# Strassen-style weight sums by accumulating DMAs, and a 32-byte place for the first weight tile, in a two-layer encoder trunk

## The chip, the cores and the metric

The kernel runs on one core of a Trainium2 chip. The metric is the device time of one execution in microseconds (us). Before the change three runs took 2366.21, 2369.56 and 2368.86 us, median 2368.86 us. For a kernel of this length a difference of under 0.2% (about 5 us) can't be told from none.

## What is computed

Two layers; each is a feed-forward block (FFN), a mixer of three branches (banded attention, pooling, forgetting attention) and another FFN, on a sequence of 512 tokens of width 1024, in float32. The change lies in the FFNs:

```python
def swiglu(h, w_gate, w_up, w_down):
    return (jax.nn.silu(h @ w_gate) * (h @ w_up)) @ w_down
...
x = x + 0.5 * mod[:, 2][:, None, :] * swiglu(h, ffn_w_gate[l, 0], ffn_w_up[l, 0], ffn_w_down[l, 0])
```

`w_gate` and `w_up` are 1024x2816, `w_down` is 2816x1024, so that the middle width of 2816 makes 22 units of 128 columns.

## The kernel before

**Products.** Activations lie transposed (features on the 128 partitions, 512 tokens in a row). Every float32 operand is split into a rounded high part (a ScalarE copy, in the traces an ACT `CAST`) and a low part (a VectorE subtraction, a DVE `TENSOR_TENSOR`), and a product is three matmuls: high by high, high by low, low by high. The weights are the stationary operand, loaded anew for each matmul (PEld), the activations the moving one. The split is `split_to` (lines 417 and 418) or, in `wchunk`, lines 310 and 312.

**FFN stages.** The 22 units of an FFN go in three parts, of 6, 8 and 8 units; after each part the part's share of `w_down` follows (`k_outer`, 512 columns wide, and in the last half of the last part 256 wide, "split"). In the first part of an FFN all or four of the six units are made the plain way (512 columns wide, `Ffn.unit`). All others go in pairs by `seven`.

**`seven`.** Two units of `w_gate`, or of `w_up`, make a 1024x256 block, which is cut in 2x2 sub-blocks A11, A12, A21, A22; the activations are cut likewise, in B11 to B22. The Winograd form of Strassen's rule needs seven products of sub-blocks in place of eight, each of four steps of 128 and three matmuls 256 wide: 84 matmuls. For it the weights are summed as S1 = A21 + A22, S2 = S1 - A11, S3 = A11 - A21 and S4 = A12 - S2, and the activations, once for an FFN, as T1 to T4 (class `Blocks`). The products run in the order A11·B11, A12·B21, S2·T2, S1·T1, S3·T3, S4·B22, A22·T4, on three PSUM banks x, y and w. Between them ACT copies a bank out (lines 572, 576, 578, 580) and DVE sums the copies (the `tens` rows of 256 elements). S2·T2, S1·T1, S3·T3 and A22·T4 add to a bank that holds an earlier product, so the copy of the bank must have been made before.

A pair of units is one `seven` for `w_gate` (PSUM tag `acc`), then one for `w_up` (tag `mm`). There are eleven stretches of such work, eight of four pairs (8 calls) and three of a single pair (2 calls), 70 calls in all.

**Loads and buffers.** The two halves of a block come by two DMAs of 512 KB each on SP's queue into `raw` (2 buffers; line 547). DVE makes the four sums of 128x512 (lines 549 and 486) into two `v2` tiles. The splits of A11/A12 and of A22 go into `w` tiles (3 buffers), those of S1/S2 and S3/S4 into two `ptb` tiles (2 buffers). A `ptb` tile is free when PE has made its two products.

**Place.** `duo` puts a weight tile at an offset (`place`, in floats) in its buffer: `WIDE` (0) for 512-wide matmuls, `NARROW` (16 floats, 64 bytes) for 256-wide ones; the `ptb` tiles lie 64 bytes off too, by small pad tiles. The moving operands begin on multiples of 256 bytes.

**Order.** The program is traced in Python, and the framework's scheduler then orders the instructions of each engine by a model of its own; on the chip each engine runs its list strictly in order, and waits for semaphores.

Of the kernel before, what the change touches and what calls it, by code (L numbers as in the profile page):

```python
# [15 lines left out]
F32 = mybir.dt.float32  # L16
F32R = mybir.dt.float32r
I32 = mybir.dt.int32
AF = mybir.ActivationFunctionType
# [3 lines left out]
P = 128  # L23
# [17 lines left out]
def encoder_kernel(tc, xT, c, w_ada, b_ada, gains, w_gate, w_up, w_down, w_qkv, w_f, w_ubg,  # L41
# [374 lines left out]
    def split_to(hi, lo, src):  # L416
        nc.scalar.copy(hi, src)  # L417
        nc.vector.tensor_tensor(lo, src, hi.bitcast(F32), op=ALU.subtract)  # L418


    def k_outer(chunk_src, nch, lhs_rhs, before_last=None):

        if before_last is None:
            parts, nheld = [(None, slice(0, T), [acc() for _ in range(4)])], 2
        else:
            parts = [(hs, slice(hs * HALF, (hs + 1) * HALF), [b((P, HALF)) for _ in range(4)])
                     for hs, b in enumerate((mmt, acc))]
            nheld = 3  # L430

        def go(part, j, chunks):
# [52 lines left out]
    def minus(o, a, b):  # L485
        nc.vector.tensor_tensor(o, a, b, op=ALU.subtract)  # L486

    class Blocks:
# [28 lines left out]

        def t1_t3(self, m):
            b1, b2 = self.full[m], self.full[m + 2]
            minus(b1[:, :, FIRST], b1[:, :, SECOND], b1[:, :, FIRST])  # L520
            minus(b1[:, :, SECOND], b2[:, :, SECOND], b1[:, :, SECOND])

        def t2_t4(self, m):
            b1, b2 = self.full[m], self.full[m + 2]
            minus(b2[:, :, SECOND], b2[:, :, SECOND], b1[:, :, FIRST])
            minus(b2[:, :, FIRST], b2[:, :, FIRST], b2[:, :, SECOND])

        def split(self, q):
            self.parts[q] = blk("b"), blk("b")
# [8 lines left out]
            q0, cols = {"T1": (0, FIRST), "T3": (0, SECOND), "T4": (2, FIRST), "T2": (2, SECOND)}[name]  # L538
            return [tuple(part[:, k % 2, cols] for part in self.parts[q0 + k // 2]) for k in range(4)]

    def seven(srcs, blocks, bank):

        raws = []
        for src in srcs:
            side_work()
            raw = st([P, KD, P], F32, "raw", NRAW)
            last["dma"] = nc.sync.dma_start(raw, src).ins
            raws.append(raw)
        tens = lambda o, a, b, op: nc.vector.tensor_tensor(o, a, b, op=op)
        a11, a12, a21, a22 = raws[0][:, :4], raws[0][:, 4:], raws[1][:, :4], raws[1][:, 4:]  # L550
        ah, al = duo((KD, P), "w", NARROW)
        split_to(ah, al, raws[0])
        bh, bl = duo((4, P), "w", NARROW)
        split_to(bh, bl, a22)
# [24 lines left out]
        go(x, "S3", "T3", False)  # L579
        nc.scalar.copy(c[:, 3], x)  # L580
# [15 lines left out]
    class Ffn:  # L596
# [19 lines left out]
        def act(self, n, pg, pu, sg=None):  # L616
            if sg is None:
                sg = apply([pg], AF.Silu)
            pr = t2(T)
            parts = pu if isinstance(pu, list) else [pu]  # L620
            m = T // len(parts)
            for i, p in enumerate(parts):
                cols = slice(i * m, (i + 1) * m)
                nc.vector.tensor_tensor(pr[:, cols], p, sg[:, cols], op=ALU.mult)
            a = blk("b")
            split_to(a[:, 0, :], a[:, 1, :], pr)
            return a

        def run(self, nxt):
# [4 lines left out]
            for part, (f0, nf) in enumerate(parts):  # L634
# [40 lines left out]
                    n += 1  # L675
                if not opening:
                    blocks.finish()
                while n < nf:
                    both = [apply(p, AF.Silu)
                            for p in seven([w_gate[l, s, f0 + n + i] for i in range(2)], blocks, acc)]  # L680
                    ups = seven([w_up[l, s, f0 + n + i] for i in range(2)], blocks, mmt)
                    for i, sg in enumerate(both):
                        acts.append(self.act(n + i, None, ups[i], sg))
                    n += 2
                MOD_RATE[0] = 1.2
                for c0 in (0, T):
# [644 lines left out]
```

## Time and profile before

| what | value |
|---|---|
| median of three runs | 2368.86 us |
| the profiled execution | 2370.22 us |
| its span on the core | 2368.4 us |
| granted TensorE clock | 1.0 |
| PE, DVE, ACT, POOL busy | 99%, 75%, 51%, 14% of the span |
| calls of `seven` | 70, in eleven stretches |
| read from HBM | 312.16 MB |

The profile is of one execution. A matmul's row begins when it begins; its end is modelled, and matmuls overlap in the pipeline, so that a busy PE says little: the distance from one matmul's start to the next is what it costs. `L418` is line 418 of the kernel, `ptb<-v` a tile of tag `ptb` written from one of tag `v2`; a group's row has its count, busy time, mean duration in ns and the idle time ahead of it, with who ended it.

### The profile page before, as it was taken

How to read it: one execution, taken by the hardware profiler on the slowest of the kernel's cores; microseconds unless marked ns; L12 is line 12 of the kernel's file. 1: busy time of each engine (PE TensorE's matmuls, PEld its weight loads, DVE VectorE, ACT ScalarE, POOL GpSimd, SP SyncE). 2: the span in 40 equal slices, each digit the busy share in tenths (PEclk: the TensorE clock that was granted, in tenths of full speed). 3: DMA queues.
4: the chain of work that ended last, by engine and by line, in shares of the span. 5: the costliest groups of instructions: out<-in, count | busy, mean ns of one | idle time of the engine just before them, and what ended most of it. 6: DMA issues, size and time to landing. Idle time of an engine off the chain costs nothing.

```text
span 2368.4 us, 37435 instructions
## 1 busy us (share of the span) xinstructions
PE 2335.2 (99%) x14322; PEld 2075.8 (88%) x14322; DVE 1770.8 (75%) x3147; ACT 1197.2 (51%) x2097; POOL 326.4 (14%) x433
## 2 busy tenths in 40 slices
PE   7999999999999999999999999999999999999999
PEld 5898998878888898989999989888788888999898
DVE  8887866787686577878687878677866855878583
ACT  5353555676632353635553536456765324636262
POOL 3000011244411100000100000112543211000000
PEclk9999999999999999999999999999999999999999
DMA  8535342333355524353415353533333654143233
GB/s 292 182 107 187 101 167 88 105 99 110 122 199 202 188 71 161 116 187 99 152 63 178 101 185 107 187 107 99 99 122 106 221 199 167 63 142 108 98 100 107
DMA packets 117976, 325.18 MB, mean 137 GB/s; under 512 B 11650, under 2 KB 13826, under 8 KB 117796
## 3 DMA queue, kind: packets, MB, share of 16 engines
q1 hardware_dynamic: 115106, 314.38, 39.9%
q0 software_dynamic: 2688, 8.39, 1.2%
q8 instruction: 113, 1.85, 0.3%
q14 instruction: 67, 0.55, 0.1%
q10 hardware_dynamic: 2, 0.00, 0.0%
HBM read 312.16 MB, written 6.38 MB: 134 GB/s over the span
## 4 chain that ended last, share of the span: by engine, by line
PE 85%; DVE 9%; ACT 3%; DMA 2%; issue 2%; SPq 0%; ACTq 0%; DVEq 0%; POOL 0%; POOLq 0%
PE acc L140 16%; PE acc L142 16%; PE acc L141 16%; PE mm L151 4%; PE mm L149 4%; PE mm L150 4%; PE acc L149 4%; PE acc L151 4%; PE acc L150 4%; PE mm L140 3%; PE mm L142 3%; PE mm L141 3%; PE mm L1020 1%; DVE w L418 1%; DVE v L486 1%
## 5 line engine op out<-in xcount | busy, mean ns | idle before, releaser
L312 DVE TENSOR_TENSOR w<-raw,w 128x1024 fp32r<-128x1024 f32 x247 | 313.2, 1271 | 161.6 <-ACT w L310 161.3
L310 ACT CAST w<-raw 128x1024 fp32r<-128x1024 f32 (+1 forms) x255 | 264.3, 1040 | 273.4 <-PE acc L142 187.5
L140 PE MATMUL acc<-b,w 128*128 128x512 f32 (+1 forms) x960 | 359.8, 375 | 0.0
L141 PE MATMUL acc<-b,w 128*128 128x512 f32 (+1 forms) x960 | 356.3, 371 | 0.0
L142 PE MATMUL acc<-b,w 128*128 128x512 f32 (+1 forms) x960 | 356.1, 371 | 0.0
L142 PEld LDWEIGHTS acc<-b,w 128*128 128x128 f32 x960 | 180.4, 188 | 31.6
L140 PEld LDWEIGHTS acc<-b,w 128*128 128x128 f32 x960 | 180.3, 188 | 30.3
L141 PEld LDWEIGHTS acc<-b,w 128*128 128x128 f32 x960 | 180.6, 188 | 29.8
L417 ACT CAST ptb<-v 128x1024 fp32r<-128x1024 f32 x140 | 146.6, 1050 | 100.8 <-DVE v L486 62.0
L418 DVE TENSOR_TENSOR ptb<-v,ptb 128x1024 fp32r<-128x1024 f32 x140 | 170.7, 1222 | 33.2 <-ACT ptb L417 32.7
L140 PE MATMUL acc<-hhi,w 128*128 128x512 f32 x480 | 191.9, 401 | 2.4 <-ACT hhi L747 1.7
L142 PE MATMUL acc<-hhi,w 128*128 128x512 f32 x480 | 188.8, 393 | 2.6 <-DVE w L312 2.6
L141 PE MATMUL acc<-hlo,w 128*128 128x512 f32 x480 | 188.7, 393 | 0.5 <-DVE hlo L750 0.5
L417 ACT CAST w<-raw 128x1024 fp32r<-128x1024 f32 (+1 forms) x140 | 116.5, 832 | 122.1 <-PE acc L142 56.2
L418 DVE TENSOR_TENSOR w<-raw,w 128x1024 fp32r<-128x1024 f32 (+1 forms) x140 | 133.1, 950 | 13.0 <-ACT w L417 13.0
L140 PE MATMUL acc<-w,hhi 128*128 128x512 f32 x336 | 138.7, 414 | 0.9 <-ACT t L849 0.9
L142 PE MATMUL acc<-w,hlo 128*128 128x512 f32 x336 | 131.9, 392 | 0.0
L141 PE MATMUL acc<-w,hhi 128*128 128x512 f32 x336 | 131.6, 392 | 0.0
L227 DVE CUSTOM_DVE_ANT_0 v<-v,b,badac 128x1024 f32<-128x1024 f32 x87 | 116.8, 1352 | 10.1 <-DMA v<-in_w_ada_dram 10.1
L149 PE MATMUL acc<-b,ptb 128*128 128x256 f32 x420 | 118.3, 282 | 0.0
L150 PE MATMUL acc<-b,ptb 128*128 128x256 f32 x420 | 117.8, 280 | 0.0
L151 PE MATMUL acc<-b,ptb 128*128 128x256 f32 x420 | 117.7, 280 | 0.0
(312 smaller groups left out, 6583.7 us busy)
## 6 DMA issues: line engine op xcount, KB each, us to landing
raw<-in_w_down_dram SPq DMA_DIRECT2D x88, 512.0 KB, 4.1
v<-in_w_ada_dram SPq DMA_DIRECT2D x87, 512.0 KB, 5.1
raw<-in_w_up_dram SPq DMA_DIRECT2D x82, 512.0 KB, 3.6
raw<-in_w_gate_dram SPq DMA_DIRECT2D x79, 512.0 KB, 3.6
b<-in_w_ada_dram SPq DMA_DIRECT2D x57, 512.0 KB, 4.7
raw<-in_w_ubg_dram SPq DMA_DIRECT2D x56, 512.0 KB, 3.6
raw<-in_w_qkv_dram SPq DMA_DIRECT2D x42, 512.0 KB, 3.7
raw<-in_w_branch_dram SPq DMA_DIRECT2D x24, 512.0 KB, 3.7
```

Of the source, the lines that this page charges most:

```text
L140: mm(o, lh, rh, start=start, stop=False)
L141: mm(o, lh, rl, start=False, stop=False)
L142: mm(o, ll, rh, start=False, stop=stop)
L149: mm(o, lh, rh, start=start and k == 0, stop=False, skip_group_check=True)
L150: mm(o, lh, rl, start=False, stop=False, skip_group_check=True)
L151: mm(o, ll, rh, start=False, stop=k == 3, skip_group_check=True)
L227: dot = nc.vector.tensor_tensor_reduce(out=raw, in0=raw, in1=silc[0], scale=1.0, scalar=badac[:, l, j, d:d + 1], op0=ALU.mult, op1=ALU.add ...
L310: nc.scalar.copy(hi, raw)
L312: lo_eng.tensor_tensor(lo, raw, hi.bitcast(F32), op=ALU.subtract)
L417: nc.scalar.copy(hi, src)
L418: nc.vector.tensor_tensor(lo, src, hi.bitcast(F32), op=ALU.subtract)
L486: nc.vector.tensor_tensor(o, a, b, op=ALU.subtract)
```

## The change

**Sums.** The signs are turned so that every weight sum is an addition: S1 = A21 + A22, S2' = S1 + A11, S3' = A11 + A21 and S4' = A12 + S2', with the T's, the SiLU's scale and the product with the second unit turned to match. A11 + A21 and A21 + A22 aren't made by DVE: SP loads A11 a second time, into the `v2` tile of S3' and S4' (`s34`, 256 KB), and A21/A22 into a tile of tag `pta` (`r1`, one buffer) in place of the second `raw`; then two DMAs on GpSimd's queue (POOL) fetch A21 and A22 from HBM once more, and add them in the place where they land (`accum_op`). DVE makes the other two sums, one of them in place in `r1`, and S1/S2' are split from `r1` itself. A call of `seven` now has two DVE sums of 128x512 for four, three SP loads (256 KB, 512 KB, 512 KB) for two, and two adding DMAs of 256 KB.

**Place.** A third place, `ENTRY`, 8 floats (32 bytes), is used for A11/A12 of the first `seven` of each stretch, and for the first chunk of a split `k_outer`; all else stays at 64 bytes.

**Order.** The lists of all engines come out otherwise, as the prediction shows.

```diff
-    WIDE, NARROW = 0, 16
+    WIDE, ENTRY, NARROW = 0, 8, 16
...
-            hi, lo = wchunk(chunk_src(c), (2, T), place=WIDE if before_last is None else NARROW)
+            hi, lo = wchunk(chunk_src(c), (2, T), place=WIDE if before_last is None else NARROW if c else ENTRY)
...
-            minus(b1[:, :, FIRST], b1[:, :, SECOND], b1[:, :, FIRST])
+            minus(b1[:, :, FIRST], b1[:, :, FIRST], b1[:, :, SECOND])
...
-            minus(b2[:, :, SECOND], b2[:, :, SECOND], b1[:, :, FIRST])
-            minus(b2[:, :, FIRST], b2[:, :, FIRST], b2[:, :, SECOND])
+            for half, other in ((SECOND, b1[:, :, FIRST]), (FIRST, b2[:, :, SECOND])):
+                t = b2[:, :, half]
+                nc.vector.scalar_tensor_tensor(t, other, -1.0, t, op0=ALU.mult, op1=ALU.subtract)
...
-    def seven(srcs, blocks, bank):
-
-        raws = []
-        for src in srcs:
-            side_work()
-            raw = st([P, KD, P], F32, "raw", NRAW)
-            last["dma"] = nc.sync.dma_start(raw, src).ins
-            raws.append(raw)
+    def seven(srcs, blocks, bank, place=NARROW):
+
+        top, low = srcs
+        s34 = st([P, 2, 4, P], F32, "v2", 4)
+        side_work()
+        nc.sync.dma_start(s34[:, 0], top[:, :4])
+        r0 = st([P, KD, P], F32, "raw", NRAW)
+        last["dma"] = nc.sync.dma_start(r0, top).ins
+        side_work()
+        r1 = st([P, 2, 4, P], F32, "pta", 1)
+        last["dma"] = nc.sync.dma_start(r1.rearrange("p a k c -> p (a k) c"), low).ins
+        nc.gpsimd.dma_start(s34[:, 0], low[:, :4], accum_op=ALU.add)
+        nc.gpsimd.dma_start(r1[:, 0], low[:, 4:], accum_op=ALU.add)
...
-        s12, s34 = st([P, 2, 4, P], F32, "v2", 4), st([P, 2, 4, P], F32, "v2", 4)
-        tens(s12[:, 0], a21, a22, ALU.add)
-        minus(s34[:, 0], a11, a21)
-        minus(s12[:, 1], s12[:, 0], a11)
-        minus(s34[:, 1], a12, s12[:, 1])
+        tens(r1[:, 1], r1[:, 0], r0[:, :4], ALU.add)
+        tens(s34[:, 1], r1[:, 1], r0[:, 4:], ALU.add)
         pair12, pair34 = duo((2, 4, P), "ptb"), duo((2, 4, P), "ptb")
-        split_to(*pair12, s12)
+        split_to(*pair12, r1)
         split_to(*pair34, s34)
...
+                if sign == 1.0:
+                    nc.vector.tensor_tensor(pr[:, cols], p, sg[:, cols], op=ALU.mult)
+                else:
+                    nc.vector.scalar_tensor_tensor(pr[:, cols], p, sign, sg[:, cols], op0=ALU.mult, op1=ALU.mult)
...
+                place = ENTRY
                 while n < nf:
-                    both = [apply(p, AF.Silu)
-                            for p in seven([w_gate[l, s, f0 + n + i] for i in range(2)], blocks, acc)]
+                    gates = seven([w_gate[l, s, f0 + n + i] for i in range(2)], blocks, acc, place)
+                    place = NARROW
+                    both = [apply(p, AF.Silu, scale=sign) for p, sign in zip(gates, (1.0, -1.0))]
```

In the prediction, "gate" and "up" are the two calls of `seven` of a pair; the gate call's banks are of tag `acc`, the up call's of tag `mm`. DVE's sum of 256 elements that reads a call's bank w can be made only when that call's product S4·B22 is done; the prediction calls it the w sum.

The list of VectorE (DVE) before, in the first stretch of the first FFN: what stands between an up call (banks `mm_267` to `mm_269`, sums in `v2_270`) and the gate call after it (`raw_275` and `raw_276`, sums in `v2_279` and `v2_280`, split into `ptb_282`).

```order
L549 TENSOR_TENSOR v2_279_1733<-raw_276_1725 128x512
L418 TENSOR_TENSOR w_277_1727<-raw_275_1723,w_277_1727 128x1024
L549 TENSOR_TENSOR v2_270_1620<-mm_268_1618,v2_270_1620 128x256
L418 TENSOR_TENSOR w_278_1730<-raw_276_1725,w_278_1730 128x512
L486 TENSOR_TENSOR v2_280_1734<-raw_275_1723,raw_276_1725 128x512
L486 TENSOR_TENSOR v2_279_1733<-v2_279_1733,raw_275_1723 128x512
L486 TENSOR_TENSOR v2_280_1734<-raw_275_1723,v2_279_1733 128x512
L418 TENSOR_TENSOR ptb_282_1740<-v2_279_1733,ptb_282_1740 128x1024
L549 TENSOR_TENSOR v2_270_1620<-v2_270_1620 128x256
L549 TENSOR_TENSOR v2_270_1620<-mm_269_1619,v2_270_1620 128x256
L624 TENSOR_TENSOR t2_271_1712<-v2_270_1620,t1_253_1586 128x512
```

All four sums of the gate call and the low part of S1/S2 (`ptb_282`) stand ahead of the up call's last sums (`v2_270` from `mm_269`, which is bank w with S4·B22).

The same place of DVE's list after the change: the up call's banks are now `mm_261` to `mm_263` and its sums `v2_264`; the gate call's `r1` is `pta_271`, its `s34` is `v2_269` and its S1/S2' are split into `ptb_275`; `w_289` holds A11/A12 of the up call after that.

```order
L555 TENSOR_TENSOR v2_264_1620<-mm_263_1619,v2_264_1620 128x256
L627 TENSOR_TENSOR t2_265_1712<-v2_264_1620,t1_248_1586 128x512
L629 SCALAR_TENSOR_TENSOR t2_267_1717<-v2_264_1620,t1_249_1588 128x256
L555 TENSOR_TENSOR pta_271_1727<-pta_271_1727,raw_270_1725 128x512
L418 TENSOR_TENSOR b_266_1714<-t2_265_1712,b_266_1714 128x512
L629 SCALAR_TENSOR_TENSOR t2_267_1717<-mm_261_1617,t1_249_1588 128x256
L555 TENSOR_TENSOR v2_269_1723<-pta_271_1727,raw_270_1725 128x512
L418 TENSOR_TENSOR w_289_1857<-raw_287_1851,w_289_1857 128x1024
L418 TENSOR_TENSOR b_268_1720<-t2_267_1717,b_268_1720 128x512
L418 TENSOR_TENSOR ptb_275_1740<-pta_271_1727,ptb_275_1740 128x1024
```

The gate call's first sum (`pta_271`) and all that hangs on it have moved behind the up call's S4·B22 sum, and six rows stand between that sum and the low part `ptb_275`.

The turn from the gate call to the up call of one pair, DVE's list after the change: `v2_247` and the bank `acc_246` are the gate call's, `pta_252`, `v2_250` and `ptb_256` the up call's.

```order
L555 TENSOR_TENSOR v2_247_1494<-acc_246_1493,v2_247_1494 128x256
L555 TENSOR_TENSOR pta_252_1595<-pta_252_1595,raw_251_1593 128x512
L555 TENSOR_TENSOR v2_250_1591<-pta_252_1595,raw_251_1593 128x512
L418 TENSOR_TENSOR ptb_256_1608<-pta_252_1595,ptb_256_1608 128x1024
L555 TENSOR_TENSOR v2_264_1620<-mm_262_1618,v2_264_1620 128x256
```

Here, too, the call's sum stands right behind the S4·B22 sum of the call before it.

SP's list after the change, around the same calls: `raw` tiles are `r0`, `v2` tiles `s34`, `pta` tiles `r1`.

```order
L549 DMA raw_270_1725<-in_w_gate_dram 128x1024
L547 DMA v2_250_1591<-in_w_up_dram 128x512
L552 DMA pta_252_1595<-in_w_up_dram 128x1024
L547 DMA v2_269_1723<-in_w_gate_dram 128x512
L549 DMA raw_287_1851<-in_w_up_dram 128x1024
L552 DMA pta_271_1727<-in_w_gate_dram 128x1024
```

The `r1` load of a call (`pta_271`) has only one buffer to go to, so it waits until the call before has read its own (`pta_252`, last read by the low part `ptb_256`), while `r0` is loaded two calls ahead.

More of the change, by code (lines that the diff above doesn't have):

```diff
@@ L539, in operand @@
             return [tuple(part[:, k % 2, cols] for part in self.parts[q0 + k // 2]) for k in range(4)]
-    def seven(srcs, blocks, bank):
-        raws = []
-        for src in srcs:
-            side_work()
-            raw = st([P, KD, P], F32, "raw", NRAW)
-            last["dma"] = nc.sync.dma_start(raw, src).ins
-            raws.append(raw)
+    def seven(srcs, blocks, bank, place=NARROW):
[10 more added lines that the diff above has]
+        nc.gpsimd.dma_start(r1[:, 0], low[:, 4:], accum_op=ALU.add)
         tens = lambda o, a, b, op: nc.vector.tensor_tensor(o, a, b, op=op)
-        a11, a12, a21, a22 = raws[0][:, :4], raws[0][:, 4:], raws[1][:, :4], raws[1][:, 4:]
-        ah, al = duo((KD, P), "w", NARROW)
-        split_to(ah, al, raws[0])
+        ah, al = duo((KD, P), "w", place)
+        split_to(ah, al, r0)
         bh, bl = duo((4, P), "w", NARROW)
-        split_to(bh, bl, a22)
-        s12, s34 = st([P, 2, 4, P], F32, "v2", 4), st([P, 2, 4, P], F32, "v2", 4)
-        tens(s12[:, 0], a21, a22, ALU.add)
-        minus(s34[:, 0], a11, a21)
-        minus(s12[:, 1], s12[:, 0], a11)
-        minus(s34[:, 1], a12, s12[:, 1])
+        split_to(bh, bl, r1[:, 1])
+        tens(r1[:, 1], r1[:, 0], r0[:, :4], ALU.add)
+        tens(s34[:, 1], r1[:, 1], r0[:, 4:], ALU.add)
         pair12, pair34 = duo((2, 4, P), "ptb"), duo((2, 4, P), "ptb")
-        split_to(*pair12, s12)
+        split_to(*pair12, r1)
         split_to(*pair34, s34)
@@ L614, in unit, with act @@
                        k == 0, k == KD - 1)
-        def act(self, n, pg, pu, sg=None):
+        def act(self, n, pg, pu, sg=None, sign=1.0):
             if sg is None:
@@ L623, in act @@
                 cols = slice(i * m, (i + 1) * m)
-                nc.vector.tensor_tensor(pr[:, cols], p, sg[:, cols], op=ALU.mult)
+                if sign == 1.0:
+                    nc.vector.tensor_tensor(pr[:, cols], p, sg[:, cols], op=ALU.mult)
+                else:
+                    nc.vector.scalar_tensor_tensor(pr[:, cols], p, sign, sg[:, cols], op0=ALU.mult, op1=ALU.mult)
             a = blk("b")
@@ L677, in run @@
                     blocks.finish()
+                place = ENTRY
                 while n < nf:
-                    both = [apply(p, AF.Silu)
-                            for p in seven([w_gate[l, s, f0 + n + i] for i in range(2)], blocks, acc)]
+                    gates = seven([w_gate[l, s, f0 + n + i] for i in range(2)], blocks, acc, place)
+                    place = NARROW
+                    both = [apply(p, AF.Silu, scale=sign) for p, sign in zip(gates, (1.0, -1.0))]
                     ups = seven([w_up[l, s, f0 + n + i] for i in range(2)], blocks, mmt)
                     for i, sg in enumerate(both):
-                        acts.append(self.act(n + i, None, ups[i], sg))
+                        acts.append(self.act(n + i, None, ups[i], sg, (1.0, -1.0)[i]))
                     n += 2
```

## The prediction

> **What bounds the kernel now.** I read the page first, then the windows of the eleven stretches of `seven`, then the groups by form for what PE waits on there, then PE alone in two quiet windows. The page's engine rows and chain:
>
> ```profile
> span 2368.4 us, 37435 instructions
> PE 2335.2 (99%) x14322; PEld 2075.8 (88%) x14322; DVE 1770.8 (75%) x3147; ACT 1197.2 (51%) x2097; POOL 326.4 (14%) x433
> PE 85%; DVE 9%; ACT 3%; DMA 2%; issue 2%; SPq 0%; ACTq 0%; DVEq 0%; POOL 0%; POOLq 0%
> ```
>
> PE never rests for long; the chain goes through DVE for 9% of the span, in stages that this alone doesn't tell. The windows by stretch (start:end, length, then busy time and instructions of PE, PEld, DVE, ACT, POOL, the clock, the DMA engines' share, GB/s):
>
> ```profile
> 123.60:202.80 79.20, 78.96 (x673) 78.73 (x672) 69.51 (x105) 46.64 (x80) 0.00 (x0) 1.00 0.42 133
> 246.30:325.40 79.10, 78.42 (x673) 78.13 (x673) 69.18 (x106) 46.51 (x80) 0.00 (x0) 1.00 0.40 128
> 946.10:1025.30 79.20, 78.71 (x673) 78.47 (x672) 69.00 (x103) 46.61 (x80) 0.00 (x0) 1.00 0.41 132
> 1068.90:1147.90 79.00, 78.46 (x674) 78.19 (x673) 69.44 (x107) 46.40 (x81) 0.00 (x0) 1.00 0.40 130
> 1290.50:1370.70 80.20, 79.11 (x674) 78.63 (x673) 69.03 (x103) 46.22 (x80) 0.00 (x0) 1.00 0.41 130
> 1414.20:1494.00 79.80, 78.66 (x673) 77.90 (x672) 68.44 (x105) 46.07 (x80) 0.00 (x0) 1.00 0.40 128
> 2117.70:2197.90 80.20, 78.86 (x673) 78.27 (x673) 66.81 (x101) 46.33 (x80) 0.00 (x0) 1.00 0.36 113
> 2241.50:2320.50 79.00, 79.00 (x674) 78.90 (x673) 66.83 (x101) 46.50 (x81) 0.00 (x0) 1.00 0.35 114
> sum 695.30, PE 689.77 PEld 686.62 DVE 597.35 ACT 401.52 POOL 0.00; mean PE 62.71 PEld 62.42 DVE 54.30 ACT 36.50 POOL 0.00
> ```
>
> These are the eight stretches of four pairs, and the sum over all eleven. The eight come to 635.7 us, 19.87 us a pair. DVE is busy for 86% of the time, and PE idles for 695.30 - 689.77 = 5.5 us in all. What ends that idle time:
>
> ```profile
> L149 PE MATMUL acc<-b,w 128*128 128x256 f32 x140 | 40.7, 290 | 4.5 <-ACT v L580 4.5
> L149 PE MATMUL mm<-b,w 128*128 128x256 f32 x140 | 39.3, 281 | 1.0 <-ACT v L580 1.0
> ```
>
> It is ACT's copy of bank x ahead of A22·T4, which stands behind a split that waits for DVE's sums. So relief of DVE can win back 5.5 us there and no more. The rest is PE's pace. Two windows of 18 us without a wait, early and late in one stretch:
>
> ```profile
> 1080.00:1098.00 18.00, 18.00 (x156) 1.00 0.28 88
> 1117.60:1135.60 18.00, 18.00 (x162) 1.00 0.26 94
> ```
>
> A row lasts 0.28 us and counts where it overlaps the window, so a matmul costs 18.28/156 = 0.117 us in the first and 18.28/162 = 0.113 us in the second, at the same clock, with the same shapes and places. Two paces exist. Between the windows lies this, on PE (start, length):
>
> ```profile
> 1116.84 0.28 PE L151 MATMUL acc<-hhi,ptb 128*128 128x256 f32 x1
> 1116.98 0.39 PE L149 MATMUL acc<-b,w 128*128 128x256 f32 x1
> 1117.21 0.28 PE L150 MATMUL acc<-b,w 128*128 128x256 f32 x1
> 1117.32 0.28 PE L151 MATMUL acc<-b,w 128*128 128x256 f32 x1
> ```
>
> Starts of 0.14 and 0.23 us apart, at the first matmul of A22·T4: a small wait, after which the pace is the faster one.
>
> **The place.** The split `k_outer`, too, begins slow; the window on the first one's first 16 us gives 16.28/137 = 0.119:
>
> ```profile
> 347.30:363.30 16.00, 16.00 (x137) 1.00 0.40 132
> ```
>
> If 32 bytes in the first tile start a stretch in the fast pace, each first pair gains 168 x 0.004 = 0.7 us, eleven times, and each of six split `k_outer`s 137 x 0.005 = 0.7 us: 12 us. (Later pairs are counted below at the fast pace anyway, on the estimate that any wait brings it as that one did.) Every 256-wide tile of `seven` lies at 64 bytes in both windows, so no row shows what 32 does; bounds 0 and -12, I take the middle, -6.
>
> The Trainium skill, "TensorE: Matmul & The Clock Gate", section "Step-by-step: what each phase is for", says that PE has two independent SBUF read ports, so that loading the next weights takes no read bandwidth from the running matmul. By it a weight tile's place beside the moving operand would be worth nothing, and the sum below 6 us more. The two windows neither bear it out nor refute it: the pace changes there with the places left as they are.
>
> **The adding DMAs and DVE's rows.** Durations:
>
> ```profile
> L417 ACT CAST ptb<-v 128x1024 fp32r<-128x1024 f32 x140 | 146.6, 1050 | 100.8 <-DVE v L486 62.0 <-ACT v L580 15.4 <-PE mm L151 11.9
> L418 DVE TENSOR_TENSOR ptb<-v,ptb 128x1024 fp32r<-128x1024 f32 x140 | 170.7, 1222 | 33.2 <-ACT ptb L417 32.7 <-PE acc L151 0.4
> L486 DVE TENSOR_TENSOR v<-raw,raw 128x512 f32<-128x512 f32 x70 | 47.9, 684 | 0.0
> L418 DVE TENSOR_TENSOR b<-t,b 128x512 fp32r<-128x512 f32 x88 | 59.5, 684 | 0.1
> L549 DVE TENSOR_TENSOR v<-mm,v 128x256 f32<-128x256 f32 x70 | 29.2, 418 | 1.1 <-PE mm L151 1.1
> L592 ACT ACTIVATE t<-v 128x512 f32<-128x512 f32 x35 | 22.1, 632 | 3.5 <-DVE v L549 3.2
> L592 ACT ACTIVATE t<-v 128x256 f32<-128x256 f32 x35 | 14.3, 408 | 0.0
> ```
>
> Removed: two DVE sums a call, 2 x 0.68 us, 2.7 us a pair. Of that only the 5.5 us can show, since DVE isn't what PE waits for. The new `scalar_tensor_tensor` rows are few (16 for the T's, two of 256 elements a pair) and take what their neighbours take, within a tenth; I count 0.42 for each of the two. The second A11 load and the adding DMAs take a call's traffic from 1 to 1.75 MB and the DMA share from 0.42 to about 0.73: still room.
>
> Moved: DVE's first sum of a call now stands behind the w sum of the call before, which waits for S4·B22 there. I count from S, the end of S4·B22, at the fast pace of 0.113.
>
> Gate to up: w sum 0.42, then the S2' sum 0.68 on DVE, while ACT makes two SiLU pieces, 0.63 and 0.41, and only then the split: its cast ends at 0.42 + 0.63 + 0.41 + 1.05 = 2.5 us, the low part 1.22 later, at 3.7. PE meanwhile has 24 matmuls to make in its list (12 of A22·T4, 8 left of A12·B21, 4 that need the high part alone): 2.7 us. It waits 1.0 us.
>
> Up to gate: w sum 0.42, the two products with the SiLU 0.69 and 0.42, so the S2' sum starts at 1.5. From there to the end of `ptb`'s low part stand seven rows, 0.68 + 0.68 + 0.42 + 0.68 + 1.22 + 0.68 + 1.22 = 5.6; successive DVE rows start about 0.08 before the last one's end,
>
> ```profile
> 1324.27 0.68 DVE L418 TENSOR_TENSOR w<-raw,w 128x512 fp32r<-128x512 f32 x1
> 1324.87 0.69 DVE L486 TENSOR_TENSOR v<-raw,raw 128x512 f32<-128x512 f32 x1
> ```
>
> so 6.6 in all. PE has 56 matmuls (12, then 24 of the gate call, and 20 others put ahead): 6.3. It waits 0.3.
>
> So by order alone a pair takes 168 x 0.113 = 19.0, plus 1.3: 20.3 us.
>
> Added: the round of `r1`'s one buffer. It is free at the end of the low part; then SP loads it, POOL's queue adds to it, and only then can DVE's S2' sum run. Rows for the prices, and the landing times of line 547's loads in all stretches:
>
> ```profile
> raw<-in_w_gate_dram SPq DMA_DIRECT2D x79, 512.0 KB, 3.6
> x_dram<-xv POOLq DMA_DIRECT2D x8, 512.0 KB, 3.1
> b<-b POOLq DMA_DIRECT2D x32, 128.0 KB, 2.2
> DMA to landing us min/median/max: 3.4/3.6/5.8
> ```
>
> The load: 3.6, or about 4.0 where `r0` was issued just ahead of it (the gate call's). The adding DMA, X, isn't in the trace. A plain one of 256 KB lies between the 128 KB and the 512 KB rows of POOL's queue, 2.2 + 0.9 x 128/384 = 2.5; I take 2.4 as the low bound. An adding one must fetch its destination too; twice the moving part of the 256 KB gives 3.1, four times it 4.3, my upper bound. I take 3.0, near the doubling.
>
> Gate's S2' sum: by `r1` at 3.7 + 4.0 + X = 10.7 after the gate call's S before it. By order: the up call ends S4·B22 44 matmuls (5.0 us) after the low part, at 8.7, and the sum starts 1.5 later, at 10.2. `r1` is 0.5 late. Up's S2' sum: by `r1` at 6.6 + 3.6 + 3.0 = 13.2; by order 6.6 + 5.0 + 0.42 = 12.0. 1.2 late. A pair takes 20.3 + 1.7 = 22.0 us, against 19.87: 2.1 more. With X = 2.4 it is 20.9, with 4.3 it is 24.6.
>
> This holds from the second pair of a stretch on, since the first finds its loads made: three pairs in each of eight stretches, 24 x 2.1 = 50 us. First pairs of those eight pay the gate-to-up wait of 1.0: 8 us. In the three single pairs the sum stands ahead of the w sum, no cost.
>
> **Sum.** 50 + 8 - 6 = 52 us on the profiled 2370.22: 2422. The median of the runs is 1.4 under that execution, so **2421 us**. Ends of this case: X = 2.4 and the place at its best, 24 + 8 - 12 = 20, 2389; X = 4.3 and no place effect, 113 + 8 = 121, 2490.
>
> **Rivals.**
> *Faster, by the pace.* The stretches run through at 0.113 from the first matmul, and the adding DMAs hide. Eight stretches of 672 x 0.113 = 75.9 us instead of 635.7/8 = 79.5 give 28 us, the single pairs 3, the splits 4: 35 us, 2334. It decides at a pair under 19.87, that is where order and `r1` together cost PE under 0.9 us a pair. For it: the late window runs so for 18 us, and DVE loses 2.7 us a pair, its slack grows. Against: the order's waits come out at 1.3 even with X at nothing.
> *A wash,* the two within 0.2%: waits of about 0.9 to 1.1 a pair, 2364 to 2373.
> *Slow adding.* The DMA engines add at a small part of their copying rate, or POOL's queue lags, X of 5.5: gate 3.0 late, up 3.7, a pair of 27.0, 24 x 7.1 = 171 more, 2540. For it: nothing in the trace has such a DMA. Against: the share of DMA time is low.
> *The place does nothing:* the forecast's sum with 0 for -6, 2427, in its range.
>
> **How the numbers follow.** Forecast 0.64, faster by the pace 0.17, a wash 0.07, slow adding 0.12. A measurement of this kernel can tell about 0.2%, 5 us, from no change. Faster 0.18 (the pace and a sliver of the rest), same 0.07, slower 0.75. The range goes from 2340, which leaves out most of the pace's rival, to 2500, which leaves out most of the slow adding. The forecast's own range is 2389 to 2490.
>
> **What would show it.** Right: PE's idle time in the eight stretches grows from a few us to some 50 or more, and stands before the first matmul that needs `ptb`'s low part in each call; DVE's row of the S2' sum in `pta` is ended by the adding DMA, from the second pair on by 0.5 and 1.2 us; X, from issue to landing, is near 3.0; a later pair lasts 22 us; outside the stretches nothing changes but the splits' pace. Wrong: pairs under 20 us, or an adding DMA under 2.4, or S2' sums that wait on PE alone. The place is right if the first matmuls after a 512-wide one come at 0.113, wrong at 0.117.

## The result and the profile after

The changed kernel takes 2582.41 us (median of 2582.26, 2584.11, 2574.19 and 2582.57), the kernel before 2368.04 us in the median of the runs beside it: a ratio of 1.0899, 95% interval 1.0874 to 1.0923. The sign of the forecast was right; its size, +52 us, was a quarter of the +214 us that came. The profiled execution took 2582.26 us, 212.0 more than that of before. The page's engine rows and chain:

```profile
span 2580.5 us, 37809 instructions
PE 2412.8 (94%) x14322; PEld 2127.9 (82%) x14322; DVE 1694.9 (66%) x3007; ACT 1192.3 (46%) x2097; POOL 449.3 (17%) x573
PE 60%; DMA 20%; DVE 11%; issue 5%; ACT 4%; POOLq 0%; SPq 0%; ACTq 0%; DVEq 0%
```

DVE has less to do, as intended, and the chain that ended last now goes through DMAs for 20% of the span in place of 2%. The windows on the eleven stretches of `seven`, the columns as before (two long stretches, one of a single pair, the sum over all eleven):

```profile
124.40:227.30 102.90, 87.40 (x674) 84.25 (x673) 65.70 (x96) 48.01 (x82) 12.11 (x14) 0.93 0.60 156
270.60:377.20 106.60, 90.14 (x674) 86.59 (x673) 64.90 (x97) 47.62 (x82) 11.22 (x13) 0.90 0.54 139
...
sum 907.90, PE 768.86 PEld 741.40 DVE 563.95 ACT 413.33 POOL 102.91; mean PE 69.90 PEld 67.40 DVE 51.27 ACT 37.58 POOL 9.36
```

The stretches take 907.9 us in place of 695.3, which is the whole loss: what lies outside them takes 1674 us in both traces (span less stretches, from first start to last start: 1673.8 after and 1674.5 before). Inside them PE idles for 907.90 - 768.86 = 139 us where it idled for 5.5, and the granted clock of a long stretch falls to between 0.90 and 0.95. By PE's rows a later pair lasts 26.71 us (24 of them; 19.89 before), the first pair of a long stretch 24.54 (8; 19.79), a single pair 23.5 (3; 19.8): 24 x 6.82 + 8 x 4.75 + 3 x 3.7 = 213 us. What PE waits for:

```profile
L149 PE MATMUL mm<-b,ptb 128*128 128x256 f32 x420 | 143.8, 344 | 86.6 <-ACT ptb L417 86.6
L151 PE MATMUL mm<-b,ptb 128*128 128x256 f32 x420 | 139.0, 345 | 15.9 <-DVE ptb L418 15.4
L149 PE MATMUL acc<-b,ptb 128*128 128x256 f32 x420 | 118.6, 283 | 10.9 <-ACT ptb L417 10.6
```

The same rows before, without any wait:

```profile
L149 PE MATMUL mm<-b,ptb 128*128 128x256 f32 x420 | 117.4, 279 | 0.0
L151 PE MATMUL mm<-b,ptb 128*128 128x256 f32 x420 | 117.2, 279 | 0.0
L149 PE MATMUL acc<-b,ptb 128*128 128x256 f32 x420 | 118.3, 282 | 0.0
```

PE waits for the splits into `ptb`, above all in the up call (`mm`); the next view shows it for that of S1/S2'. One round of `r1`'s buffer, in order of time, from the low part of an up call to the S2' sum of the gate call after it:

```profile
139.01 1.23 DVE L418 TENSOR_TENSOR ptb<-pta,ptb 128x1024 fp32r<-128x1024 f32 x1 [0.43 <-ACT ptb L417]
...
140.27 0.33 SPq L552 DMA_DIRECT2D pta<-in_w_gate_dram  x1
...
145.66 0.86 POOL L554 DMA_DIRECT2D pta<-in_w_gate_dram  x1 [1.27 <-DMA pta<-in_w_gate_dram]
...
150.21 0.69 DVE L555 TENSOR_TENSOR pta<-pta,raw 128x512 f32<-128x512 f32 x1 [1.20 <-DMA pta<-in_w_gate_dram]
```

Each row starts as soon as the one before it lets go: the low part ends at 140.24, the load is issued at 140.27; it lands, and the adding DMA is issued at 145.66; that lands at 150.18, and the sum starts at 150.21. In 57 of the 59 calls that aren't the first of a stretch the S2' sum starts within 0.1 us of the landing of its adding DMA. So the calls run at the pace of this round, and PE, DVE and ACT wait for it in turn. The DMA rows of the page (KB each, median us from issue to landing; SPq the loads, POOLq the adding ones):

```profile
pta<-in_w_gate_dram SPq DMA_DIRECT2D x35, 512.0 KB, 4.6
pta<-in_w_up_dram SPq DMA_DIRECT2D x35, 512.0 KB, 3.7
...
pta<-in_w_gate_dram POOLq DMA_DIRECT2D x35, 256.0 KB, 4.6
...
pta<-in_w_up_dram POOLq DMA_DIRECT2D x35, 256.0 KB, 4.2
```

So the prediction's X, from the issue of the adding DMA to its landing, is 4.2 to 4.6 us; in the 59 calls its mean is 4.33. And PE alone, right behind a wait in the first stretch:

```profile
139.03 0.39 PE L149 MATMUL mm<-b,ptb 128*128 128x256 f32 x1 [1.81 <-ACT ptb L417]
139.25 0.28 PE L150 MATMUL mm<-b,ptb 128*128 128x256 f32 x1
140.29 0.58 PE L151 MATMUL mm<-b,ptb 128*128 128x256 f32 x1 [0.76 <-DVE ptb L418]
140.67 0.42 PE L149 MATMUL mm<-b,ptb 128*128 128x256 f32 x1
140.89 0.41 PE L150 MATMUL mm<-b,ptb 128*128 128x256 f32 x1
141.10 0.41 PE L149 MATMUL mm<-b,ptb 128*128 128x256 f32 x1
```

After the waits matmuls start 0.213 us apart in place of 0.113, for some 3 us. That is half clock: the clock granted from 140.8 to 143.2 us is 0.50. The stretches have 617 starts at about this distance, 23 before; some 480 of them stand in 31 spells of 8 or more, the others are single or in twos. Sorted by the distance to the next start, the stretches' 212.7 us more are 163 of waits, 60 of these 617 starts (48 of it in the spells), and 11 less from pace.

The Trainium skill, "TensorE: Matmul & The Clock Gate", section "What's actually happening", says that one idle window of about 3.4 us puts the array to 1.2 GHz, half of its rate, and that the windows run freely. The trace agrees on the half rate, and on windows that run freely: spells of 15 or 16 starts (3.2 us) are the commonest, and of two single pairs with waits of 3.18 and 3.04 us the one with the longer wait shows no spell. It doesn't agree that it takes an idle window of that length: ahead of 25 of the 31 spells the longest distance between two starts is under 3.4 us, and the one shown here follows two of 2.08 and 1.04 us.

### The profile page after: what moved, and what is told of

Read it like the earlier page. It is cut to its first block, busy times and chain, and to the rows that moved or that the text cites. A ratio compares the mean times of both kernels' runs of the same rounds, so it can differ in the third digit from the quotient of the medians.

```text
span 2580.5 us, 37809 instructions
## 1 busy us (share of the span) xinstructions
PE 2412.8 (94%) x14322; PEld 2127.9 (82%) x14322; DVE 1694.9 (66%) x3007; ACT 1192.3 (46%) x2097; POOL 449.3 (17%) x573
## 4 chain that ended last, share of the span: by engine, by line
PE 60%; DMA 20%; DVE 11%; issue 5%; ACT 4%; POOLq 0%; SPq 0%; ACTq 0%; DVEq 0%
PE acc L140 14%; PE acc L142 14%; PE acc L141 14%; DMA pta<-in_w_up_dram 11%; DMA pta<-in_w_gate_dram 7%; PE mm L140 3%; DVE ptb L418 3%; PE mm L142 3%; PE mm L141 3%; DVE pta L555 2%; PE mm L151 2%; PE mm L149 2%; ACT ptb L417 2%; PE mm L150 1%; PE mm L1027 1%
## 5 line engine op out<-in xcount | busy, mean ns | idle before, releaser
L310 ACT CAST w<-raw 128x1024 fp32r<-128x1024 f32 (+1 forms) x255 | 264.4, 1041 | 270.2 <-PE acc L142 176.2
L149 PE MATMUL mm<-b,ptb 128*128 128x256 f32 x420 | 143.8, 344 | 86.6 <-ACT ptb L417 86.6
L149 PEld LDWEIGHTS mm<-b,ptb 128*128 128x128 f32 x420 | 103.8, 247 | 92.9 <-ACT ptb L417 92.9
L418 DVE TENSOR_TENSOR w<-pta,w 128x512 fp32r<-128x512 f32 x70 | 48.5, 693 | 189.9 <-ACT w L417 189.9
L151 PE MATMUL mm<-b,ptb 128*128 128x256 f32 x420 | 139.0, 345 | 15.9 <-DVE ptb L418 15.4
L150 PE MATMUL mm<-b,ptb 128*128 128x256 f32 x420 | 139.2, 333 | 0.0
L467 DVE SCALAR_TENSOR_TENSOR xv<-acc,badac,xv 128x512 f32<-128x512 f32 (+1 forms) x112 | 77.4, 691 | 90.2 <-PE acc L142 90.0
L149 PE MATMUL acc<-b,ptb 128*128 128x256 f32 x420 | 118.6, 283 | 10.9 <-ACT ptb L417 10.6
```

Of the source, the lines that this page charges most:

```text
L149: mm(o, lh, rh, start=start and k == 0, stop=False, skip_group_check=True)
L150: mm(o, lh, rl, start=False, stop=False, skip_group_check=True)
L151: mm(o, ll, rh, start=False, stop=k == 3, skip_group_check=True)
L310: nc.scalar.copy(hi, raw)
L467: nc.vector.scalar_tensor_tensor(x, acc_j, gate, x, op0=ALU.mult, op1=ALU.add)
```

## The experiments

Two theories stood against each other. The loop: one buffer for `r1` ties low part, load, adding DMA and S2' sum into a ring, and the ring's length is the time of a call. The rival: adding DMAs cost by themselves wherever they stand, by the DMA engines' or POOL's time, or by the clock that falls. Times below are medians, ratios are to the kernel before, beside it on the same chip; "stretches" is the sum of the windows on the eleven stretches.

**The place alone**, on the kernel before.

```diff
-    WIDE, NARROW = 0, 16
+    WIDE, ENTRY, NARROW = 0, 8, 16
...
+        place=WIDE if before_last is None else NARROW if c else ENTRY
...
+        ah, al = duo((KD, P), "w", place)
```

> The kernel before with the 32-byte place alone (first call of each stretch, first chunk of each split). If the place works as the trace after suggests (every entry goes from 118 to 113 ns a matmul after about 24 matmuls, and stays there until something brings 118 back): the excess over 113 ns in the eleven stretches falls from 20.5 us to some 6, that of the splits from 4.2 to some 2, and the time is 2352 us, 15 under the kernel before (12 to 18). If the fast pace after the change came from the waits of the adding DMAs and not from the place: 2368, no change, and entries stay at 118.

2362.57 us, 0.9979 (0.9970 to 0.9988): about 5 us gained, a third of what was expected of the pace. The first 16 us of the first stretch, before:

```profile
123.60:139.60 16.00, 16.00 (x137) 15.98 (x136) 13.32 (x20) 8.73 (x16) 0.00 (x0) 1.00 0.31 100
```

and with the place:

```profile
124.50:140.50 16.00, 16.00 (x142) 16.00 (x141) 13.40 (x20) 9.14 (x17) 0.00 (x0) 1.00 0.32 101
```

142 matmuls in place of 137: 16.28/142 = 0.115. The stretches ran 15.4 us less over 113 ns (5.1 for 20.5), and took 4.6 us less in all; most of the difference came back as waits at the copy of bank x, for which PE waited 4.5 us before:

```profile
L149 PE MATMUL acc<-b,w 128*128 128x256 f32 x140 | 41.5, 296 | 11.4 <-ACT v L580 11.1
```

**The place at 128 bytes**, on the kernel before.

```diff
-    WIDE, ENTRY, NARROW = 0, 8, 16
+    WIDE, ENTRY, NARROW = 0, 32, 16
```

> The place alone on the kernel before, at 128 bytes in place of 32. In the run with 32 bytes the tile at 32 bytes itself still ran at 118 and 117 ns a matmul, and 113 came with the first tile after it, at 64. If the step from one place to another turns the pace: entries again go to 113 after the first tile, 2360 to 2364 us. If it takes 32 bytes: entries stay at 118, 2367.

2363.14 us, 0.9982 (0.9972 to 0.9991), and ten of the eleven entries go to 113 after the first tile too (the third single pair stays at 0.120). With 32 bytes the first tile's 24 matmuls took 2.84 us at the fifth stretch (0.118 each), with 128 bytes 2.89 us (0.120), and what follows at 64 bytes comes at 0.113. So the step from one place to another turns the pace, with either place, and the tile at 32 bytes itself is no faster than one at 64. Why the step does so stays open.

**Signs and place**, all four sums by DVE from two `raw` tiles.

```diff
-        nc.gpsimd.dma_start(s34[:, 0], low[:, :4], accum_op=ALU.add)
-        nc.gpsimd.dma_start(r1[:, 0], low[:, 4:], accum_op=ALU.add)
...
+        tens(s12[:, 0], a21, a22, ALU.add)
+        tens(s34[:, 0], a11, a21, ALU.add)
```

> The changed kernel with all four sums made by DVE from two raw tiles, as before the change: signs and place alone. If the turned signs cost nothing: 2362 us, as the place alone. If the two products by scalar_tensor_tensor or the other order of DVE's list cost 1 us a pair: 2397.

2360.58 us, 0.9974 (0.9963 to 0.9985). The signs cost nothing.

**One buffer for `r1`, no adding DMA.** As the changed kernel, but DVE makes all sums, two of them in `r1`.

```diff
-        nc.sync.dma_start(s34[:, 0], top[:, :4])
...
+        tens(s34[:, 0], r0[:, :4], r1[:, 0], ALU.add)
+        tens(r1[:, 0], r1[:, 0], r1[:, 1], ALU.add)
```

> The changed kernel with r1 in its one buffer, but no adding DMA and no second load of A11: DVE makes all four sums. It prices the one buffer and the order that comes of it without any adding DMA. If the S3' adding DMA is hidden, as the loop theory has it, this is as slow as the run with that adding DMA alone (2417): 2405 to 2425, a pair 21 to 21.5 us. If that adding DMA was what cost there, 2365 to 2385.

2410.97 us, 1.0182 (1.0165 to 1.0199): 50 us over signs and place. A piece of the chain of waits in the first stretch (start, us, what):

```profile
158.15 4.45 DMA pta<-in_w_gate_dram
...
162.63 0.70 DVE v L552
163.32 0.65 DVE w L418
163.97 0.61 DVE pta L552
...
164.61 0.69 DVE pta L552
165.30 1.27 DVE v L552 x3
166.57 1.14 DVE ptb L418
167.73 4.26 DMA pta<-in_w_up_dram
```

The ring is there without any adding DMA: load 4.3 us, then DVE's rows down to the low part. At 10.0 us a turn (mean of 59 calls; 9.6 in the first one shown) it is no shorter than what PE needs for a call (19.9 us a pair before), and a pair lasts 21.1 us.

**The S3' adding DMA alone** (S1 by DVE in `r1`, one buffer).

```diff
-        nc.gpsimd.dma_start(r1[:, 0], low[:, 4:], accum_op=ALU.add)
+        tens(r1[:, 0], r1[:, 0], r1[:, 1], ALU.add)
```

> The changed kernel with S3' = A11+A21 by an adding DMA as there, but S1 = A21+A22 made by DVE in r1, one buffer as there. The loop theory: the loop then holds one load and one DVE sum of 0.69 us in place of load and adding DMA, about 18 us a pair, below what PE needs, and the S3' adding DMA has a buffer long before: a pair of 20 to 20.6 us, the time 2370 to 2390. If adding DMAs cost wherever they stand (by contention or POOL's queue), half of the loss stays: about 2475.

2416.68 us, 1.0206 (1.0189 to 1.0223). More than I expected of the loop, but only 6 us more than one buffer alone: this adding DMA costs little there, and I had priced the ring without it too low.

**The adding DMA into `r1` alone.** DVE makes S3' as S2' - A22, so that S1 and S3' share a `ptb` tile, and S2' and S4' the other.

```diff
-        nc.sync.dma_start(s34[:, 0], top[:, :4])
...
-        nc.gpsimd.dma_start(s34[:, 0], low[:, :4], accum_op=ALU.add)
...
-        tens(r1[:, 1], r1[:, 0], r0[:, :4], ALU.add)
-        tens(s34[:, 1], r1[:, 1], r0[:, 4:], ALU.add)
+        tens(s34[:, 0], r1[:, 0], r0[:, :4], ALU.add)
+        tens(r1[:, 1], s34[:, 0], r1[:, 1], ALU.subtract)
+        tens(s34[:, 1], s34[:, 0], r0[:, 4:], ALU.add)
```

> The changed kernel with the adding DMA into r1 alone: S3' is made by DVE as S2' - A22, so that the S3' adding DMA and the second load of A11 are gone (the traffic of a call falls from 1.75 to 1.25 MB, the adding DMAs from 140 to 70). The loop theory: the loop is as in the changed kernel plus one DVE sum of 0.69 us a call, 26.3 + 1.4 = 27.7 us a pair, and the time is 2600 to 2640 us. If adding DMAs cost by their number, by traffic or by POOL's queue: about half of the loss, 2470.

2565.56 us, 1.0836 (1.0820 to 1.0853). With half the adding DMAs, and a third of the added traffic, nearly all of the loss stays. (It came out 34 us under the loop's low end: a ring lasts 13.1 us, as in the changed kernel, not the 13.9 that one more DVE sum would make of it. The adding DMA lands a little sooner, 4.0 to 4.2 us in the median.) The windows' sum over the eleven stretches:

```profile
sum 889.70, PE 782.39 PEld 741.58 DVE 573.45 ACT 417.13 POOL 54.51; mean PE 71.13 PEld 67.42 DVE 52.13 ACT 37.92 POOL 4.96
```

**Plain copies for adding ones**, in the same places. The kernel leaves out the sums A11 + A21 and A21 + A22.

```diff
-        nc.gpsimd.dma_start(r1[:, 0], low[:, 4:], accum_op=ALU.add)
+        nc.gpsimd.dma_start(r1[:, 0], low[:, 4:])
```

> The changed kernel with both of GpSimd's DMAs made plain copies of the same bytes to the same places (the sums A11+A21 and A21+A22 are left out). It measures what adding costs against copying, in place. The loop theory: a plain one lands in about 2.5 us against 4.3, two a pair in the loop, so a pair falls from 26.3 to 22.6 us, a long stretch to about 91 us, the time to about 2480 us (2460 to 2500). If the half-speed matmuls are a cost of their own, the gain is larger, since waits of under 3 us leave fewer of them: 2440 or less. If adding is no dearer than copying on POOL's queue: no change, 2580.

2503.68 us, 1.0568 (1.0552 to 1.0584). The DMA rows of the page:

```profile
pta<-in_w_gate_dram POOLq DMA_DIRECT2D x35, 256.0 KB, 2.9
...
pta<-in_w_up_dram POOLq DMA_DIRECT2D x35, 256.0 KB, 2.9
```

2.9 us copying against 4.2 to 4.6 adding (means of 59 calls 2.98 and 4.33): adding costs 1.35 us more for 256 KB. With 2.98 in place of the 2.5 I had guessed, the ring gives 24.1 us a pair; 24.5 were measured. So the time follows the ring, and plain DMAs in these places would still have lost 136 us.

**Two buffers for `r1`**, both adding DMAs, room taken from `t2`.

```diff
-        r1 = st([P, 2, 4, P], F32, "pta", 1)
+        r1 = st([P, 2, 4, P], F32, "pta", 2)
...
-        return st([P, cols], F32, "t2", 3)
+        return st([P, cols], F32, "t2", 1)
```

> The changed kernel with two buffers for r1 in place of one (the room comes from the t2 tiles, three buffers made one). The loop theory: in the changed kernel a call can't be shorter than S2' to low part, then load 4.1 us, 0.56 to the issue, adding DMA 4.3, which is 26.3 us a pair; with two buffers that loop spans two calls and is hidden, so that a pair falls to the 20.3 us that order alone gives, the eight long stretches last 80 to 84 us in place of 103 to 106, and the time is about 2385 us (2365 to 2410). If adding DMAs cost by sharing the DMA engines or POOL's queue, or if the half-speed matmuls were a cost of their own, more than 2450.

2494.33 us, 1.0538 (1.0524 to 1.0552): the stretches fell from 907.9 to 788.6 us, a little over half of the way. That is far from the forecast. The wait that stayed, by ACT's list of waits:

```profile
ACT ptb L417 <- DMA v<-in_w_gate_dram: 94.4, 22, 8.2
```

ACT's split of S3'/S4' waits for the other adding DMA (into `v`, the tag of `s34`). Where it stands, in the order of time:

```profile
159.97 0.33 SPq L552 DMA_DIRECT2D pta<-in_w_up_dram  x1
...
160.34 0.43 SPq L547 DMA_DIRECT2D v<-in_w_gate_dram  x1
...
164.06 0.86 POOL L554 DMA_DIRECT2D pta<-in_w_up_dram  x1 [12.42 <-DMA pta<-in_w_up_dram]
164.59 1.22 POOL L553 DMA_DIRECT2D v<-in_w_gate_dram  x1
```

The `v` DMA stands behind the one into `pta` of the next call, and so do their loads in SP's list, in 49 of the 70 calls. By the trace it is SP's order that makes it late: the load at 160.34 goes out right behind the `pta` load, and that waited for its buffer, whose last reader on DVE ends at 159.94. POOL's order adds nothing: in the 35 calls in which the trace has the landing of the `v` load, POOL issues the adding DMA 0.53 us after it in the median, 0.66 at most, no longer than where nothing stands ahead (0.56). And with both adding DMAs issued within 0.6 us, the one into `v` lands 5.7 us after its issue in the median, where it took 4.2 in the changed kernel. A new wait had taken the place of the one removed.

**Two buffers with one adding DMA each.** The kernels with the adding DMA into `r1` alone and into `s34` alone, each with

```diff
-        r1 = st([P, 2, 4, P], F32, "pta", 1)
+        r1 = st([P, 2, 4, P], F32, "pta", 2)
...
-        return st([P, cols], F32, "t2", 3)
+        return st([P, cols], F32, "t2", 1)
```

> The adding DMA into r1 alone (S3' by DVE as S2' - A22) with two buffers for r1 and one for t2. The run with both adding DMAs and two buffers lost 127 us still, which the loop through r1 doesn't explain; there ACT's split waited for the S3' adding DMA, and that stands in POOL's list behind an adding DMA into r1 that waits for its load. If the loop and POOL's order are the whole cost: here both are gone, and the time is 2365 to 2400 us. If the adding DMA into r1 costs by itself (DMA engines, its latency in each call): 2450 or more.

> The S3' adding DMA alone (S1 by DVE) with two buffers for r1 and one for t2. If the rest of the loss with two buffers came from POOL's order (the S3' adding DMA behind the one into r1): gone here, 2362 to 2390 us, and the 50 us of the one buffer, which the run with this adding DMA and one buffer paid, are gone too. If it came from the S3' adding DMA's own chain (its load stands in SP's list behind r1's, its buffer is one of the four v2): 2440 or more.

2408.64 us, 1.0170 (1.0153 to 1.0187), with the adding DMA into `r1`; 2419.98 us, 1.0225 (1.021 to 1.024), with the one into `s34`. Neither time is as forecast, but the stretches are what tells. The sum of the windows with the adding DMA into `r1`:

```profile
sum 694.00, PE 693.78 PEld 688.97 DVE 576.27 ACT 422.23 POOL 55.24; mean PE 63.07 PEld 62.63 DVE 52.39 ACT 38.38 POOL 5.02
```

From 889.7 to 694.0 us by the second buffer (and the lists that come out of it), PE idle for 0.2 us in all (by the distances of the starts some 4 us of waits, 7 before): the same 70 adding DMAs, no faster (4.1 and 5.2 us), make PE wait for nothing where the ring spans two calls. With the `s34` one the stretches take 714.2 us (744.1 with one buffer), with both 788.6. SP's order is as it was (the `s34` load behind the next call's `r1` load in 49 calls), and ACT's split waits for this adding DMA though no other stands on POOL's queue; it lands in 4.0 us in the median here, 5.7 beside the other one. So SP's order and the slower landing fit what stayed with both; no run changed the order alone. The rest of the loss is outside the stretches, 1703 to 1720 us there.

**The control for `t2`**: signs and place, with one `t2` buffer.

```diff
-        return st([P, cols], F32, "t2", 3)
+        return st([P, cols], F32, "t2", 1)
```

> Signs and place, all sums by DVE, with one t2 buffer in place of three: the control for the runs with two buffers for r1, whose room came from t2. If t2 is what made these runs slower outside the stretches of seven (1703 and 1720 us there, against 1672 with the place alone): 2390 to 2400 us, with the stretches at 689 as without it. If the two buffers or the adding DMAs did it: 2361, no change against signs and place.

2393.83 us, 1.0108 (1.0092 to 1.0123), stretches 690.0 us, outside 1702.7 (1671.1 with three `t2` buffers). So 31 us of the runs with two buffers are `t2`'s; some 18 us more, outside the stretches with the adding DMA into `r1`, stay unexplained (its profiled execution, 2414.94 us, is itself 6 us over the median).

**S3 by POOL**, on the kernel with the place alone.

```diff
-        minus(s34[:, 0], a11, a21)
+        nc.gpsimd.tensor_tensor(s34[:, 0], a11, a21, op=ALU.subtract)
```

> The kernel before with the place, and S3 = A11 - A21 computed by GpSimd (a POOL TENSOR_TENSOR of 128x512 takes 1.61 to 1.66 us in the trace before, where DVE takes 0.68) in place of DVE. With the place alone, the eleven stretches gained 15 us of pace and lost 10 of them again to waits for DVE's and ACT's work, 18.1 us in all. If DVE's load is what makes these waits: they fall to some 5 us, and the time is 2348 us (2344 to 2354). If POOL's sum slows DVE beside it, or its own 1.6 us comes too late: 2362 or more.

2388.70 us, 1.0091 (1.0076 to 1.0106), 26 us more than with the place alone. DVE's low part of A11/A12 beside POOL's sum:

```profile
L418 DVE TENSOR_TENSOR w<-raw,w 128x1024 fp32r<-128x1024 f32 x70 | 137.0, 1957 | 7.2 <-ACT w L417 7.2
```

and with the place alone:

```profile
L418 DVE TENSOR_TENSOR w<-raw,w 128x1024 fp32r<-128x1024 f32 x70 | 85.3, 1219 | 4.8 <-ACT w L417 4.8
```

It grows from 1.22 to 1.96 us, 52 us in all, more than the 48 of DVE's work that went to POOL: the 57 of these rows that run beside POOL's sum take 2.13 us in the mean, the other 13 1.22. The Trainium skill, "SBUF — State Buffer", section "Who interferes with whom", says that a DVE instruction with two SBUF inputs contends with a GpSimd one that reads SBUF; here it does.

**No shared buffer.** The adding DMA into `r1` alone, the gate call's `r1` in `pta`, the up call's in the `strip` tiles, `t2` with two buffers, and the 32-byte place in every call.

```diff
+    def seven(srcs, blocks, bank, place=NARROW, home=("pta", 1)):
...
+        r1 = st([P, 2, 4, P], F32, *home)
...
+                    ups = seven([w_up[l, s, f0 + n + i] for i in range(2)], blocks, mmt, ENTRY, ("strip", 2))
```

> A version that may beat both kernels: the adding DMA into r1 alone (S3' by DVE as S2' - A22), the gate call's r1 in the pta tile, the up call's in the two strip tiles, made 1 KB larger each, so that no call waits for the buffer of the call before; t2 with two buffers for the room; the first tile of every call at 32 bytes, so that every call has the step from 32 to 64 that brought 113 ns. By the run with two buffers (11 stretches in 694 us, 4.5 us of waits, 21.9 us over 113 ns): pace falls to some 10 us, the stretches to 682 us; outside them 1672 us as with the place alone, or some 15 more for t2: 2353 to 2370 us. If the adding DMA into r1 costs even with a buffer of its own: 2400 or more.

2363.76 us, 0.9985 (0.9976 to 0.9994). The sum of the windows:

```profile
sum 684.10, PE 684.10 PEld 679.90 DVE 577.39 ACT 421.80 POOL 50.87; mean PE 62.19 PEld 61.81 DVE 52.49 ACT 38.35 POOL 4.62
```

PE doesn't idle in the stretches at all, with 70 adding DMAs in them; with one shared buffer the same adding DMAs made them 889.7 us. Two ways of giving `r1` more room, each with lists of its own, took the waits away, and in both the adding DMAs stayed; so the shared buffer is the cause of the loss. The time is 0.15% under the kernel before, too little to call it faster, and no better than the place alone or signs and place; the three intervals overlap.

## Why the prediction was right in sign and wrong in size

Step by step, from signs and place (2360.6 us): the one buffer costs 50 us, the S3' adding DMA 6, the adding DMA into `r1` 166.

*What bounds the kernel* was right: without a shared buffer PE idles for 0.0 us of the 5.5, and the rest is pace. *Signs and T's at nothing*: right. *Nothing outside the stretches but the splits' pace*: right.

*The round of `r1`'s one buffer* was the right mechanism, with its price too low. In the prediction's terms a later pair was S2' sum to low part 3.28 (3.7 - 0.42) and 5.1 (6.6 - 1.5), loads 4.0 + 3.6, and 2 x 3.0 for X, 22.0 us. Means over the 24 later pairs, call of up and call of gate:

| term of a later pair, us | predicted | measured |
|---|---|---|
| S2' sum to low part | 8.4 | 3.07 + 4.99 = 8.06 |
| issue of the load to issue of the adding DMA | 7.6 | 4.41 + 5.18 = 9.59 |
| X | 6.0 | 4.48 + 4.32 = 8.80 |
| landing to sum, end of low part to load | 0 | 0.26 |
| pair | 22.0 | 26.7 (26.7 in PE's rows) |

So the step that failed first is "I take 3.0, near the doubling": X lies at what the sum had as its upper bound, 4.3, for which it gave 24.6 a pair. The other 2 are the hand-overs between the queues, at nothing in the sum (twice 0.56 us from the landing of a load to the issue of its adding DMA, 0.26 for the rest), and longer loads. PE had nothing in hand to cover them, so each counted in full, 24 times: 24 x 4.7 = 113 of the 162 us by which the forecast fell short.

Two more steps failed outright. "The first finds its loads made" holds for the gate call alone: the up call's `r1` needs the buffer that the gate call holds until its low part, so the first pairs paid 4.75 us, not 1.0, and the single pairs 3.7, where the sum said "no cost" because it had looked at the order there and not at the ring. Together 41 us. And the slow clock wasn't in the sum. In a later pair it costs nothing of its own: the ring accounts for the whole pair, and no link of it waits for PE (from S2' sum to low part pass 3.07 to 3.08 us in every up call and 4.76 to 5.10 in every gate call, from low part to load at most 0.07), so that slow matmuls only fill part of a wait. At the end of a stretch it seems to cost: of the three single pairs two had 17 or 18 starts at half clock, and took 24.1 us where the third took 22.4.

The waits "by order" (1.0 and 0.3 a pair) weren't found by themselves: with the adding DMA into `r1` and two buffers, PE idled for 0.2 us over all eleven stretches, though DVE's list came out otherwise there too, so that this isn't settled for the order of the changed kernel.

*The place* was taken at -6 and measured -5, which is luck: by the prediction's own test (first matmuls at 0.113) it was wrong, since they come at 0.118. The step to another place turns the pace and wins 15 us in the stretches, more than the 12 that the prediction allowed, and some 10 of them are waited away again. The Trainium skill, "TensorE: Matmul & The Clock Gate", section "Step-by-step: what each phase is for", would make the place worth nothing, by its two independent read ports; the runs with 32 and 128 bytes show a small gain.

Of the rivals, slow adding had the mechanism with X at 5.5; from the landing of a load to the S2' sum 0.56 + 4.33 + 0.09 = 5.0 us pass, nearer to that than to 3.0. The faster rival fell on the ring. A range to 2500 left out the first pairs' ring, and what the small terms add up to when nothing hides them.

## What to carry to other kernels

Follow every single buffer once around, from its last reader through the load, each further DMA and the engines back to that reader, and hold the sum against the time of one turn of the work: latencies that are free with a second buffer are all on the path without it, and so are the hand-overs between queues. Do it for the first turn too. And when a wait is removed, read what stands next in the in-order queues: a load behind another that waits for its buffer is as late as that one.

## What the runs showed of the hardware

An adding DMA of 256 KB from HBM into SBUF lands 4.2 to 4.6 us after its issue in the changed kernel's medians (3.8 at least, 8.2 at most), a plain one on the same queue in 2.9 to 3.2, and its issue holds POOL for 0.86 us against 0.54. From the landing of a load to POOL's issue of the DMA that waited for it pass 0.56 us. Matmuls 256 wide start 0.213 us apart at half clock, and half clock came after two distances of 2.08 and 1.04 us between starts. At the start of a stretch, with the weight tile 128 bytes off they start 0.120 us apart, 32 bytes off 0.118, and 64 bytes off 0.113 or 0.118, by what went before. A low part by DVE of 128x1024 took 2.13 us beside a sum by POOL, and 1.22 without.
